# Pace and order of the S5 output work beside the gate projection, and the row pitch of its short kernels in DRAM

## The chip, the cores and the metric

The kernel runs on one core of one Trainium2 chip. A core has a matrix engine (TensorE, PE, with its weight loads PEld on a side path), a vector engine (VectorE, DVE), an activation engine (ScalarE, ACT), a general engine (GpSimd, POOL), and a queue engine (SyncE, SP) that issues most of the transfers between DRAM and on-chip memory (SBUF); matrix products collect in banks of PSUM. The metric is the time of one execution on the device in microseconds, the median of several runs.

## The reference

The program is a trunk of two sub-layers over 256 frames of width 2048: a gated linear attention and an S5 layer, each with modulation by a condition vector, a SiLU gate branch, an output projection and a LayerNorm. The change is in the S5 mixer alone:

```python
proj = u_in @ w_in                        # 2048 -> 2 x 4096
u, z = jnp.split(proj, 2, axis=-1)
...                                       # lb, bb: the discretised diagonal A and B
def blk(args):                            # 16 groups of 16 channels, 64 complex states each
    u_b, lr_b, li_b, br_b, bi_b, cr_b, ci_b = args
    bu_r = jnp.einsum('blgi,gpi->blgp', u_b, br_b)
    bu_i = jnp.einsum('blgi,gpi->blgp', u_b, bi_b)
    ...
    _, _, x_r, x_i = lax.associative_scan(_linear_recurrence_combine, (a_r, a_i, bu_r, bu_i), axis=1)
    return jnp.einsum('blgp,gip->blgi', x_r, cr_b) - jnp.einsum('blgp,gip->blgi', x_i, ci_b)
y = lax.map(blk, ...) + d_skip * uf
y = jax.nn.gelu(y)
y = y * jax.nn.sigmoid(y @ w_glu + b_glu)
y = y * jax.nn.silu(z)
return y @ w_out
```

All inputs and the output are float32.

## The kernel before

**Precision.** Each float32 weight tile is split into a high part `hi` (an ACT cast, line 145) and a low part `lo` (a DVE subtraction, line 146), and each product is made of three matmuls: high by high, high by low, low by high (lines 180, 181 and 182 in `st_step`; `u1h` and `u1l` are the parts of the layer's input, already in SBUF).

**The stages of the S5 layer.** First `su`: the columns of u, in 8 groups of 512. Beside it run the preparation of B and C, the first half of the scan, and the making of short kernels: the response of the recurrence inside 8 frames, one 16 x 1024 block for each of 32 f tiles (an f tile is 128 channels, 8 groups of 16). `k_out` writes these to a scratch array `dk` in DRAM, rows of 1920 floats, 16 rows for each f tile. Then comes `sz`: the gate columns z, again in 8 groups g of 8 steps kp; a step loads 512 KB of weights (`wload`, through SP; a ring of four tiles `wsz`), splits them (rings of three `hisz` and three `losz`) and issues 24 matmuls into four PSUM banks. The pool `mm` has five banks, so that a group's banks must be read by its four SiLUs (line 1280, `zs`) before the next group can go far. Last come `gl` (the GLU projection, lines 192 and 193, which needs y of all f tiles from its first step on), the output projection and the LayerNorm.

**The background list.** During groups 1 to 7 of `sz`, 56 steps, the program also finishes the scan's second half and makes y. A list `bg` holds closures; after each step's matmuls `pump(Y_RATE)` adds 2.311 to an account and calls one closure for each whole 1.0 in it. The closures are:

- `scan(cidx, 1)`, 30 of them: one step of the recurrence over chunks of 8 frames for the second half of the channels. Three DVE instructions, each needing the one before: a product (line 1183, into `sca`), a sum (1184), and a sum into the states `sx` (1185).
- `cside(f)`, 32 of them: `cload(f + 1)` issues three transfers of C and the powers of A (`cl`, two buffers, lines 1213 and 1215); `mload(f)` issues one transfer of 512 KB that spreads the short kernel of f from `dk` into a banded matrix `mt` (two buffers, line 1229): partition (i, s) reads 1024 consecutive floats of row i, beginning 128 floats later for each s. `cunit(f)` makes C times the powers, two DVE products (lines 1074 and 1075, tiles `wc`, two buffers each).
- `xstage(f)`: the states at the chunk starts, transposed by DVE (line 1237, `xT`, one buffer) and by PE (line 1240, `psxs`), and copied by ACT to `xS` (line 1242).
- `ystage(f)`: 24 small matmuls on PE into `psy`, 8 with `mt` on the inputs U (line 1252) and 16 with `wc` on the states `xS` (line 1255); then a DVE transpose `yt` (line 1258) and an ACT GELU that writes y over U (line 1259).

Tiles 16 to 31 belong to the scan's second half, which has to be complete before `xstage(16)`. For each f from 0 to 33 the list has up to three scans, then `cside(f)`, `xstage(f - 1)` and `ystage(f - 2)`: six entries while there are scans (ten tiles), three afterwards. Thirty scans, 32 `cside`, 32 `xstage` and 32 `ystage` are 126 entries. What is left at the end of the 56 steps is called ahead of `gl`.

**What sets the order in the end.** The program text gives each engine a first order, and the tile framework then places the instructions on each engine's queue anew by their dependences, so that the pieces of one closure may be apart from one another. The engine executes its queue strictly in that order. PE's next step waits for `hisz` and `losz`; a `psy` group waits for `mt`, `wc` and `xS`; a `mt` transfer waits for the `psy` group of two tiles before, which frees the buffer; SP's queue stands while its first transfer waits. The SiLU and the GELU use different tables of ACT's functions, and each change between them is a load on ACT.

Of the kernel before, what the change touches and what calls it, by code (L numbers as in the profile page):

```python
# [8 lines left out]
F32 = mybir.dt.float32  # L9
# [24 lines left out]
def trunk(ctx, tc, x, c, ln_g, ln_b, ada_w, ada_b, gla_w_in, gla_gate_w2, gla_gate_b, gla_norm_g,  # L34
# [7 lines left out]
    def pool(name, bufs=1, **kw):  # L42
        return ctx.enter_context(tc.tile_pool(name=name, bufs=bufs, **kw))
# [9 lines left out]
    dp = pool("dram", 1, space=DRAM)  # L53
# [23 lines left out]
    def psm(name):  # L77
        return mm.tile([P, 512], F32, tag="mm", name=name)

    def psx(name):  # L80
        return ax.tile([P, 512], F32, tag="ax", name=name)
# [10 lines left out]
    bg = []  # L92
# [3 lines left out]
    def pump(rate=1.0):  # L96
        pace[0] += rate
        while pace[0] >= 1.0:
            pace[0] -= 1.0
            if bg:  # L100
                bg.pop(0)()
# [28 lines left out]
    def less(got):  # L130
        for r, b in got:
            r.drop(b)
# [330 lines left out]

    rec = dp.tile([P, 32, 384], F32, name="rec")

    dk = dp.tile([512, 1920], F32, name="dk")
    dxn = dp.tile([T, D], F32, name="dxn")
    du = dp.tile([8, P, 1024], F32, name="du")

# [219 lines left out]
    KEEP = (4, 6)  # L689
    GATE_AT = 20  # L690
    SCAN_RATE = 1.728
    Y_RATE = 2.311
    qt, kt = qk
    gl = {}

# [352 lines left out]
    def Uv(f):  # L1048
        return Ut[f // 8][:, (f % 8) // 4, :, f % 4, :]
# [161 lines left out]
    def cload(f):  # L1211
        a = tp.tile([P, 384], F32, tag="cl", name=f"cl{f}", bufs=2)
        dma(a[:, 0:256], rec[:, f, 0:256])
        for h in range(2):
            dma(a[64 * h:64 * h + 64, 256:384], rec[64 - 64 * h:128 - 64 * h, f, 0:128])
        cl[f] = a
# [7 lines left out]
    kap = dk[:, :]  # L1224

    def mload(f):
        m = tp.tile([P, 8, 8, 16], F32, tag="mt", name=f"mt{f}", bufs=2)
        src = bass.AP(tensor=kap.tensor, offset=kap.offset + f * 16 * 1920, ap=[[1920, 16], [128, 8], [1, 1024]])
        dma(m.rearrange("p t g i -> p (t g i)"), src)
        mt[f] = m  # L1230

# [2 lines left out]
    def xstage(f):  # L1234
        xt_ = tp.tile([P, 2, 4, 32], F32, tag="xt", name=f"xT{f}", bufs=1)
        n = 2 * (f % 16)
        V.transpose(xt_, sx[:, f // 16, 0:32, :, n:n + 2].rearrange("p c r b -> p b r c"))
        px = psx(f"psxs{f}")
        for b in range(2):
            PE.transpose(px[:, b * P:(b + 1) * P], xt_[:, b].rearrange("p r l -> p (r l)"), ident)  # L1240
        xs = tp.tile([P, 2, 128], F32, tag="xs", name=f"xS{f}", bufs=2)
        S.copy(xs, px[:, :T].rearrange("p (b r) -> p b r", b=2))
        xss[f] = xs

    def ystage(f):
        xs = xss[f]
        py = psx(f"psy{f}")
        U = Uv(f)
        for b in range(2):
            o = py[:, b * P:(b + 1) * P]  # L1250
            for q in range(4):
                PE.matmul(o[32 * q:32 * q + 32], lhsT=U[:, 2 * q + b], rhs=mt[f][:, :, 2 * q + b, :], start=True, stop=False)
            for w in wc[f]:
                for q in range(4):
                    PE.matmul(o[32 * q:32 * q + 32], lhsT=xs[:, b, 32 * q:32 * q + 32],
                              rhs=w[:, 2 * q + b].rearrange("p n i -> p (n i)"), start=False, stop=(w is wc[f][-1]))
        yt = tp.tile([P, 8, 32], F32, tag="yt", name=f"yt{f}", bufs=2)
        V.transpose(yt, py[:, :T].rearrange("p (b t i) -> p t b i", b=2, t=8))
        S.activation(U, yt, AF.Gelu_apprx_tanh)

    def cside(f):
        if f < 31:
            cload(f + 1)
        mload(f)
        cunit(f)

    zs = []
    for g in range(8):
        banks = [psm(f"sz{g}{f}") for f in range(4)]
        for kp in range(8):  # L1270
            w = split(wload(sw, 2 * kp, E + g * 512, f"sz{g}{kp}"), f"sz{g}{kp}")
            st_step(banks, u1, w, kp, 15)
            if g == 0:
                bstep(1 + kp % 2)
            pump(SCAN_RATE if g == 0 else Y_RATE)
        for f in range(4):
            i = (g * 4 + f) % 8
            if g % 2 == 0 and f == 0:
                zs.append(s8t(f"zs{g // 2}", [8, T]))
            S.activation(zs[g // 2][:, i, :], banks[f][:, :T], AF.Silu)  # L1280
        if g == 0:
            bstep(len(bq))
            while bg:
                bg.pop(0)()
            less(mid)
            tp.close()
            tp.open("tmp2")
            cload(0)
            sc1 = [lambda cidx=cidx: scan(cidx, 1) for cidx in range(1, 31)]
            for f in range(34):  # L1290
                for _ in range(3):
                    if sc1:
                        bg.append(sc1.pop(0))
                if f < 32:
                    bg.append(lambda f=f: cside(f))
                if 1 <= f < 33:
                    bg.append(lambda f=f: xstage(f - 1))
                if f >= 2:
                    bg.append(lambda f=f: ystage(f - 2))
    while bg:  # L1300
        pump()

    tp.close()
    rp.open("rows1")
# [147 lines left out]
```

## Time and profile before

| | before |
|---|---|
| median of 3 runs | 1825.99 us |
| lowest, highest | 1824.85, 1827.47 us |
| the profiled execution's own time | 1828.37 us |
| its span in the profile | 1826.6 us |
| mean granted clock of TensorE in it | 0.992 |
| ACT: high parts of `sz`, mean of one | 1050 ns |
| `wsz`, 512 KB, issue to landing, all 64 | 5.7 us |
| `mt`, 512 KB, issue to landing, all 32 | 7.8 us |
| `zs`, SiLU of one bank, median | 384 ns |

A row of the profile's groups names the line, the engine, the operation, the tiles written and read, the shape, and how often it occurs; then the busy time, the mean of one, and the idle time of the engine just ahead of such instructions with what ended it. A row of the waits gives the waiting instruction, what released it, and then the sum of the idle time in microseconds, the number of waits and their mean. A row of the timeline has the start in microseconds from the span's start, the duration, the engine and the instruction, `x8` for eight alike in a row, and in square brackets the idle time ahead of it. The engines' times beside each other say which one sets the pace. The matmuls of `sz` run from 1016.9 to 1277.5 us of this execution, group 0 included.

### The profile page before, as it was taken

How to read it: one execution, taken by the hardware profiler on the slowest of the kernel's cores; microseconds unless marked ns; L12 is line 12 of the kernel's file. 1: busy time of each engine (PE TensorE's matmuls, PEld its weight loads, DVE VectorE, ACT ScalarE, POOL GpSimd, SP SyncE). 2: the span in 40 equal slices, each digit the busy share in tenths (PEclk: the TensorE clock that was granted, in tenths of full speed). 3: DMA queues.
4: the chain of work that ended last, by engine and by line, in shares of the span. 5: the costliest groups of instructions: out<-in, count | busy, mean ns of one | idle time of the engine just before them, and what ended most of it. 6: DMA issues, size and time to landing. Idle time of an engine off the chain costs nothing.

```text
span 1826.6 us, 33659 instructions
## 1 busy us (share of the span) xinstructions
PE 1780.4 (97%) x13491; PEld 1573.1 (86%) x13491; DVE 1411.3 (77%) x1880; ACT 898.9 (49%) x1266; POOL 86.3 (5%) x94
## 2 busy tenths in 40 slices
PE   7999999999999999999999999999999999999997
PEld 5776897899999888799999999989888888888885
DVE  4887757879999988687789789889577775557556
ACT  4433557556556333655555544546545444444332
POOL 0000000000000000002224300000000000000000
PEclk9999999999999999999999999999999999999998
DMA  9996975879889998587666577999788886668553
GB/s 344 387 358 229 296 249 163 277 265 324 288 285 323 331 364 290 175 254 212 193 199 191 171 223 211 242 241 239 227 283 267 275 275 200 189 200 316 195 183 92
DMA packets 246101, 457.86 MB, mean 251 GB/s; under 512 B 19828, under 2 KB 49198, under 8 KB 244662
## 3 DMA queue, kind: packets, MB, share of 16 engines
q1 hardware_dynamic: 239320, 436.02, 74.4%
q0 software_dynamic: 5856, 18.63, 3.1%
q8 instruction: 106, 1.74, 0.4%
q10 hardware_dynamic: 768, 1.05, 0.2%
q14 instruction: 51, 0.42, 0.1%
HBM read 437.01 MB, written 18.61 MB: 249 GB/s over the span
## 4 chain that ended last, share of the span: by engine, by line
PE 83%; DVE 6%; DMA 5%; ACT 3%; issue 3%; SPq 1%; POOL 0%; DVEq 0%; ACTq 0%; POOLq 0%
PE gl L192 13%; PE gl L193 7%; PE op L168 6%; PE op L169 6%; PE op L167 6%; PE v L168 3%; PE z L182 3%; PE z L181 3%; PE z L180 3%; PE v L169 3%; PE v L167 3%; PE sz L180 3%; PE sz L182 2%; PE su L180 2%; PE sz L181 2%
## 5 line engine op out<-in xcount | busy, mean ns | idle before, releaser
L146 DVE TENSOR_TENSOR logl<-wgl,higl 128x1024 fp32r<-128x1024 f32 x128 | 156.7, 1224 | 116.3 <-ACT higl L145 114.6
L145 ACT CAST higl<-wgl 128x1024 fp32r<-128x1024 f32 x128 | 134.3, 1050 | 172.2 <-PE gl L192 165.4
L192 PE MATMUL gl<-yp,higl 128*128 128x512 f32 x512 | 179.9, 396 | 0.1
L192 PE MATMUL gl<-yb,higl 128*128 128x512 f32 x512 | 179.6, 396 | 0.0
L145 ACT CAST hio<-wo 128x1024 fp32r<-128x1024 f32 x95 | 100.2, 1055 | 153.0 <-PE op L169 134.8
L146 DVE TENSOR_TENSOR loo<-wo,hio 128x1024 fp32r<-128x1024 f32 x95 | 116.7, 1230 | 66.4 <-ACT hio L145 64.5
L317 DVE SCALAR_TENSOR_TENSOR acc<-wa,cs,acc 128x512 f32<-128x512 f32 x217 | 163.0, 751 | 2.7
L180 PE MATMUL su<-u1h,hisu 128*128 128x256 f32 x512 | 151.4, 297 | 0.0
L180 PE MATMUL sz<-u1h,hisz 128*128 128x256 f32 x512 | 150.1, 293 | 1.2 <-ACT zs L1280 1.2
L180 PE MATMUL z<-u0h,hiz 128*128 128x256 f32 x512 | 148.7, 290 | 0.0
L182 PE MATMUL su<-u1h,losu 128*128 128x256 f32 x512 | 145.3, 284 | 0.4 <-DVE losu L146 0.4
L182 PE MATMUL sz<-u1h,losz 128*128 128x256 f32 x512 | 144.5, 283 | 1.1 <-DVE losz L146 1.1
L182 PE MATMUL z<-u0h,loz 128*128 128x256 f32 x512 | 144.9, 283 | 0.6 <-DVE loz L146 0.6
L181 PE MATMUL su<-u1l,hisu 128*128 128x256 f32 x512 | 145.1, 284 | 0.0
L181 PE MATMUL z<-u0l,hiz 128*128 128x256 f32 x512 | 144.7, 283 | 0.0
L181 PE MATMUL sz<-u1l,hisz 128*128 128x256 f32 x512 | 144.5, 282 | 0.0
L193 PE MATMUL gl<-yb,logl 128*128 128x256 f32 x512 | 143.0, 279 | 0.0
L193 PE MATMUL gl<-yp,logl 128*128 128x256 f32 x512 | 142.3, 280 | 0.0
L145 ACT CAST hisz<-wsz 128x1024 fp32r<-128x1024 f32 x64 | 67.0, 1050 | 108.4 <-PE sz L181 60.2
L192 PEld LDWEIGHTS gl<-yp,higl 128*128 128x128 f32 x512 | 95.9, 188 | 23.3 <-issue 0.8
L192 PEld LDWEIGHTS gl<-yb,higl 128*128 128x128 f32 x512 | 96.1, 188 | 23.0
L145 ACT CAST hiz<-wz 128x1024 fp32r<-128x1024 f32 x64 | 67.2, 1052 | 89.0 <-PE z L181 79.4
(322 smaller groups left out, 5001.1 us busy)
## 6 DMA issues: line engine op xcount, KB each, us to landing
wgl<-in_s_w_glu SPq DMA_DIRECT2D x128, 512.0 KB, 4.8
wa<-in_ada_w SPq DMA_DIRECT2D x116, 512.0 KB, 5.3
wv<-in_gla_w_in SPq DMA_DIRECT2D x64, 512.0 KB, 6.2
wz<-in_gla_w_in SPq DMA_DIRECT2D x64, 512.0 KB, 5.0
wsu<-in_s_w_in SPq DMA_DIRECT2D x64, 512.0 KB, 4.2
wsz<-in_s_w_in SPq DMA_DIRECT2D x64, 512.0 KB, 5.7
wo<-in_s_w_out SPq DMA_DIRECT2D x64, 512.0 KB, 4.5
a<-in_ada_w SPq DMA_DIRECT2D x31, 1024.0 KB, 10.8
```

What stands on the lines that cost most here:

```text
L145: S.copy(hi, w)
L146: last_lo[0] = V.tensor_tensor(lo, w, hi.bitcast(F32), op=ALU.subtract).ins
L167: PE.matmul(banks[tt], lhsT=uh, rhs=hi[:, kk, :], start=(k == first), stop=False)
L168: PE.matmul(banks[tt], lhsT=uh, rhs=lo[:, kk, :], start=False, stop=False)
L169: last_mm[0] = PE.matmul(banks[tt], lhsT=ul, rhs=hi[:, kk, :], start=False, stop=(k == last)).ins
L180: PE.matmul(o, lhsT=wh, rhs=u.hi(k), start=(k == first), stop=False)
L181: PE.matmul(o, lhsT=wh, rhs=u.lo(k), start=False, stop=False)
L182: last_mm[0] = PE.matmul(o, lhsT=wl, rhs=u.hi(k), start=False, stop=(k == last)).ins
L192: PE.matmul(banks[f], lhsT=hi[:, kk, fs], rhs=u.both(k), start=(k == 0), stop=False)
L193: PE.matmul(banks[f][:, :T], lhsT=lo[:, kk, fs], rhs=u.hi(k), start=False, stop=(k == last))
L317: V.scalar_tensor_tensor(acc[0], w[:, kk, :], cs[:, k:k + 1], acc[0], op0=ALU.mult, op1=ALU.add)
```

## The change

**The pitch.** `dk` has rows of 2048 floats in place of 1920, 8192 B in place of 7680. `k_out` writes and `mload` reads the same columns as before; 128 floats at each row's end stay unused.

**The list.** Groups 1 to 7 no longer use `bg` and `Y_RATE`. A list `yq` holds pairs of a weight and a closure: scan 1.0, `xstage` 1.0, `cside` 2.5, `ystage` 2.0. The sum of all weights is 30 + 32 + 2.5 x 32 + 2 x 32 = 206, and each of the 56 steps adds 206/56 = 3.68 to an account; closures are called while the account covers the first one's weight. For each f the list has two scans in place of three, so that the scans reach to the 15th tile, and `xstage(f - 1)` now stands ahead of `cside(f)`. Group 0 is as before.

```diff
@@ -463,7 +463,7 @@
 
     rec = dp.tile([P, 32, 384], F32, name="rec")
 
-    dk = dp.tile([512, 1920], F32, name="dk")
+    dk = dp.tile([512, 2048], F32, name="dk")
     dxn = dp.tile([T, D], F32, name="dxn")
     du = dp.tile([8, P, 1024], F32, name="du")
 
@@ -689,7 +689,6 @@
     KEEP = (4, 6)
     GATE_AT = 20
     SCAN_RATE = 1.728
-    Y_RATE = 2.311
     qt, kt = qk
     gl = {}
 
@@ -1225,7 +1224,7 @@
 
     def mload(f):
         m = tp.tile([P, 8, 8, 16], F32, tag="mt", name=f"mt{f}", bufs=2)
-        src = bass.AP(tensor=kap.tensor, offset=kap.offset + f * 16 * 1920, ap=[[1920, 16], [128, 8], [1, 1024]])
+        src = bass.AP(tensor=kap.tensor, offset=kap.offset + f * 16 * 2048, ap=[[2048, 16], [128, 8], [1, 1024]])
         dma(m.rearrange("p t g i -> p (t g i)"), src)
         mt[f] = m
 
@@ -1264,6 +1263,7 @@
         mload(f)
         cunit(f)
 
+    yq, owed = [], 0.0
     zs = []
     for g in range(8):
         banks = [psm(f"sz{g}{f}") for f in range(4)]
@@ -1272,7 +1272,13 @@
             st_step(banks, u1, w, kp, 15)
             if g == 0:
                 bstep(1 + kp % 2)
-            pump(SCAN_RATE if g == 0 else Y_RATE)
+            if g == 0:
+                pump(SCAN_RATE)
+            else:
+                owed += yrate
+                while yq and owed >= yq[0][0]:
+                    owed -= yq[0][0]
+                    yq.pop(0)[1]()
         for f in range(4):
             i = (g * 4 + f) % 8
             if g % 2 == 0 and f == 0:
@@ -1288,17 +1294,16 @@
             cload(0)
             sc1 = [lambda cidx=cidx: scan(cidx, 1) for cidx in range(1, 31)]
             for f in range(34):
-                for _ in range(3):
-                    if sc1:
-                        bg.append(sc1.pop(0))
+                yq.extend((1.0, sc1.pop(0)) for _ in range(2) if sc1)
+                if 1 <= f < 33:
+                    yq.append((1.0, lambda f=f: xstage(f - 1)))
                 if f < 32:
-                    bg.append(lambda f=f: cside(f))
-                if 1 <= f < 33:
-                    bg.append(lambda f=f: xstage(f - 1))
+                    yq.append((2.5, lambda f=f: cside(f)))
                 if f >= 2:
-                    bg.append(lambda f=f: ystage(f - 2))
-    while bg:
-        pump()
+                    yq.append((2.0, lambda f=f: ystage(f - 2)))
+            yrate = sum(w_ for w_, _ in yq) / 56
+    while yq:
+        yq.pop(0)[1]()
 
     tp.close()
     rp.open("rows1")
```

Line numbers of the changed kernel are one lower than before from `KEEP` to `cunit`, since the line of `Y_RATE` is gone. The order of the matmuls of one step, the transfers' sizes and all instructions are the same in both kernels; what differs is which instruction stands behind which. In the order of PE's queue, `psy` of tile 0 stands behind step 4 instead of step 6 (steps counted from 0 in groups 1 to 7), that of tile 10 behind step 25 instead of 28, that of tile 16 behind 35 in both, and that of tile 29 behind step 54 instead of 52.

Three places in the order of the queues follow. A row gives the line, the operation, the tile written and the tiles read (numbers tell buffers of the same name apart), and the shape.

The first is DVE's queue at the start of group 1, around the first two low parts behind the last `dk` writes. Before:

```order
L146 TENSOR_TENSOR losz_11541<-wsz_11538,hisz_11540 128x1024
L1185 TENSOR_TENSOR sx<-sx,sca_11444 128x128
L1074 TENSOR_TENSOR wc_11492<-cl_11406 128x1024
L1183 TENSOR_TENSOR sca_11448<-sx,l_205 128x256
L1075 TENSOR_TENSOR wc_11493<-cl_11406 128x1024
L1184 TENSOR_TENSOR sca_11448<-sca_11448 128x128
L1074 TENSOR_TENSOR wc_11574<-cl_11486 128x1024
L1185 TENSOR_TENSOR sx<-sx,sca_11448 128x128
L1075 TENSOR_TENSOR wc_11575<-cl_11486 128x1024
L1183 TENSOR_TENSOR sca_11452<-sx,l_205 128x256
L146 TENSOR_TENSOR losz_11592<-wsz_11589,hisz_11591 128x1024
```

The same place in the changed kernel, from the second `wc` product on:

```order
L1074 TENSOR_TENSOR wc_11489<-cl_11406 128x1024
L1183 TENSOR_TENSOR sca_11448<-sca_11448 128x128
L1073 TENSOR_TENSOR wc_11543<-cl_11482 128x1024
L1184 TENSOR_TENSOR sx<-sx,sca_11448 128x128
L1074 TENSOR_TENSOR wc_11544<-cl_11482 128x1024
L1182 TENSOR_TENSOR sca_11492<-sx,l_205 128x256
L1236 STREAM_TRANSPOSE xT_11585<-sx 128x256
L1183 TENSOR_TENSOR sca_11492<-sca_11492 128x128
L146 TENSOR_TENSOR losz_11595<-wsz_11592,hisz_11594 128x1024
```

The transpose of the first f tile and one more piece of a scan have moved ahead of the second low part; the four `wc` products stand there in both.

The second is DVE's queue at steps 17 to 19 of these 56. Before, from one low part to the next:

```order
L146 TENSOR_TENSOR losz_12369<-wsz_12366,hisz_12368 128x1024
L1074 TENSOR_TENSOR wc_12199<-cl_12076 128x1024
L1075 TENSOR_TENSOR wc_12200<-cl_12076 128x1024
L1258 STREAM_TRANSPOSE yt_12274<-psy_12249 128x256
L1183 TENSOR_TENSOR sca_12277<-sx,l_205 128x256
L1184 TENSOR_TENSOR sca_12277<-sca_12277 128x128
L1185 TENSOR_TENSOR sx<-sx,sca_12277 128x128
L146 TENSOR_TENSOR losz_12435<-wsz_12432,hisz_12434 128x1024
```

In the changed kernel, behind the two `wc` products of the tile at that place and up to the next low part:

```order
L1257 STREAM_TRANSPOSE yt_12230<-psy_12205 128x256
L1184 TENSOR_TENSOR sx<-sx,sca_12263 128x128
L1236 STREAM_TRANSPOSE xT_12393<-sx 128x256
L1182 TENSOR_TENSOR sca_12267<-sx,l_205 128x256
L1183 TENSOR_TENSOR sca_12267<-sca_12267 128x128
L1184 TENSOR_TENSOR sx<-sx,sca_12267 128x128
L1182 TENSOR_TENSOR sca_12385<-sx,l_205 128x256
L1183 TENSOR_TENSOR sca_12385<-sca_12385 128x128
L1184 TENSOR_TENSOR sx<-sx,sca_12385 128x128
L1182 TENSOR_TENSOR sca_12389<-sx,l_205 128x256
L1183 TENSOR_TENSOR sca_12389<-sca_12389 128x128
L146 TENSOR_TENSOR losz_12403<-wsz_12400,hisz_12402 128x1024
```

There the two `wc` products, one `yt` and three pieces of a scan stand between two low parts; here, behind the `wc` products, it is one `yt`, one `xT` and nine pieces of scans.

The third is PE's queue at the end of the stage. Before, the last `psy` group (tile 31; its second half reads alike), the last step of `sz` (only its first three and last matmul are shown) and the first matmul of `gl`:

```order
L1252 MATMUL psy_14643<-mt_14477,U_7548 32x128 x4
L1255 MATMUL psy_14643<-wc_14479,xS_14583 32x128 x4
L1255 MATMUL psy_14643<-wc_14480,xS_14583 32x128 x4
...
L180 MATMUL sz_14218<-u1h_7422,hisz_14673 128x256
L181 MATMUL sz_14218<-u1l_7424,hisz_14673 128x256
L182 MATMUL sz_14218<-u1h_7422,losz_14674 128x256
...
L182 MATMUL sz_14221<-u1h_7422,losz_14674 128x256
L192 MATMUL gl_14721<-yp_14717,higl_14727 128x512
```

In the changed kernel, the last matmuls of the last step, then `psy` of tiles 30 and 31 (first half of each), and the first matmul of `gl`:

```order
L180 MATMUL sz_14183<-u1h_7422,hisz_14617 128x256
L181 MATMUL sz_14183<-u1l_7424,hisz_14617 128x256
L182 MATMUL sz_14183<-u1h_7422,losz_14618 128x256
L1251 MATMUL psy_14645<-mt_14473,U_7548 32x128 x4
L1254 MATMUL psy_14645<-wc_14475,xS_14542 32x128 x4
L1254 MATMUL psy_14645<-wc_14476,xS_14542 32x128 x4
...
L1251 MATMUL psy_14677<-mt_14574,U_7548 32x128 x4
L1254 MATMUL psy_14677<-wc_14576,xS_14613 32x128 x4
L1254 MATMUL psy_14677<-wc_14577,xS_14613 32x128 x4
...
L192 MATMUL gl_14721<-yp_14717,higl_14727 128x512
```

The last group of tile 31 has moved from ahead of the last step of `sz` to behind it, and that of tile 30 stands with it, right ahead of `gl`.

## The prediction

> **What bounds the kernel now.** I read the page first: TensorE (PE) is busy for almost the whole span.
>
> ```profile
> span 1826.6 us, 33659 instructions
> PE 1780.4 (97%) x13491; PEld 1573.1 (86%) x13491; DVE 1411.3 (77%) x1880; ACT 898.9 (49%) x1266; POOL 86.3 (5%) x94
> ```
>
> The change touches the stretch in which PE computes the gate columns `sz` of groups 1 to 7 (56 steps of 24 matmuls) and, between the steps, the S5 output of 32 f tiles. By the trace it runs from about 1050 to 1278 us. The table by windows splits it where the scans end:
>
> ```profile
> core 0: us, PE busy (x) PEld busy (x) DVE busy (x) ACT busy (x) POOL busy (x), PEclk, DMA share, GB/s
> 1050.00:1140.00 90.00, 87.72 (x990) 84.52 (x993) 82.66 (x150) 41.48 (x63) 2.28 (x4) 1.00 0.78 219
> 1140.00:1278.00 138.00, 135.09 (x1972) 125.91 (x1965) 122.25 (x142) 74.95 (x119) 0.00 (x0) 1.00 0.96 239
> ```
>
> PE is idle for 2.28 us in the first part and 2.91 us in the second: 5.19 us. The change leaves every matmul in place and the granted clock is already 1.00, so **5.2 us, 0.28% of the span, is the most that can be won here**. What ended this idle time is in the list of PE's waits for the same stretch:
>
> ```profile
> PE psy L1252 <- DMA mt<-dk: 1.8, 3, 1.0
> PE sz L180 <- ACT zs L1280: 1.2, 2, 1.0
> PE psy L1252 <- ACT U L1259: 1.1, 1, 1.1
> PE sz L182 <- DVE losz L146: 1.1, 1, 1.1
> ```
>
> Four kinds, then. The one on `losz` stands at the start. VectorE (DVE) comes to this stage late, held 5.2 us by the landing of the last `dk` writes, and then has 7 us of other work between two low parts:
>
> ```profile
> 1055.05 0.43 DVE L1183 TENSOR_TENSOR sca<-sx,l 128x256 f32<-128x256 f32 x1 [5.20 <-DMA dk<-ks]
> ...
> 1056.11 1.22 DVE L146 TENSOR_TENSOR losz<-wsz,hisz 128x1024 fp32r<-128x1024 f32 x1
> ...
> 1063.06 1.23 DVE L146 TENSOR_TENSOR losz<-wsz,hisz 128x1024 fp32r<-128x1024 f32 x1
> ```
>
> The two on `zs` are at group boundaries: ScalarE (ACT) has a GELU (`U`) ahead of the SiLUs that free PE's banks, the GELU waits for DVE's `yt`, and the change of function table comes on top:
>
> ```profile
> 1105.48 0.42 ACT L1259 ACTIVATE U<-yt 128x256 f32<-128x256 f32 x1 [1.41 <-DVE yt L1258]
> 1105.92 1.28 ACT L1280 ACT_TABLE_LOAD   x1
> 1107.21 1.21 ACT L1280 ACTIVATE zs<-sz 128x256 f32<-128x256 f32 x4
> ```
>
> The 1.8 us are `mt` tiles that land late, and I count the 1.1 us on `U` with them: it is at one of the same places, where an `mt` landed within a microsecond of it. The chain of waits shows two such landings after the `psy` group that freed the buffer:
>
> ```profile
> 1157.44 8.76 DMA mt<-dk
> ...
> 1235.16 7.02 DMA mt<-dk
> ```
>
> **The change part by part.** No instruction is added or removed; only order and addresses change. The unit prices are distances between starts. On PE a step's matmuls start 0.12 us apart (24 x 0.12 = 2.88 us), `psxs` takes 0.31 and a `psy` group 1.45 us, 1.76 together:
>
> ```profile
> 1268.06 0.28 PE L180 MATMUL sz<-u1h,hisz 128*128 128x256 f32 x1
> 1268.18 0.28 PE L181 MATMUL sz<-u1l,hisz 128*128 128x256 f32 x1
> ...
> 1268.42 0.38 PE L1240 MATMUL psxs<-ident,xT 128*128 128x128 f32 x2
> 1268.73 0.43 PE L1252 MATMUL psy<-mt,U 128*32 128x128 f32 x8
> ...
> 1270.18 0.38 PE L180 MATMUL sz<-u1h,hisz 128*128 128x256 f32 x1
> ```
>
> On DVE:
>
> ```profile
> 1113.11 1.21 DVE L1074 TENSOR_TENSOR wc<-cl 128x1024 f32<-128x1024 f32 x1
> 1114.24 1.21 DVE L1075 TENSOR_TENSOR wc<-cl 128x1024 f32<-128x1024 f32 x1
> 1115.38 0.44 DVE L1258 STREAM_TRANSPOSE yt<-psy 128x256 f32<-128x256 f32 x1
> 1115.75 0.38 DVE L1183 TENSOR_TENSOR sca<-sx,l 128x256 f32<-128x256 f32 x1
> ...
> 1116.69 1.22 DVE L146 TENSOR_TENSOR losz<-wsz,hisz 128x1024 fp32r<-128x1024 f32 x1
> 1117.83 0.42 DVE L1183 TENSOR_TENSOR sca<-sx,l 128x256 f32<-128x256 f32 x1
> ...
> 1118.93 0.43 DVE L1183 TENSOR_TENSOR sca<-sx,l 128x256 f32<-128x256 f32 x1
> 1119.28 0.65 DVE L1237 STREAM_TRANSPOSE xT<-sx 128x256 f32<-128x256 f32 x1
> ```
>
> A low part is 1.14, the two `wc` 2.27, `yt` 0.37, `xT` 0.58 (0.65 less the overlap of 0.07 that the others have). A scan is 0.94 (1115.75 to 1116.69) to 1.10 (1117.83 to 1118.93).
>
> *The pace.* Before, a step takes 2.311 list entries. An f tile with three scans has six entries and lasts 2.60 steps; one without has three and lasts 1.30. Now the list weighs 30 + 32 + 80 + 64 = 206, so 3.68 a step: a tile with two scans (7.5) lasts 2.04 steps, one without (5.5) 1.50.
> - With scans, DVE per tile: before 3 x 0.94 to 1.10, + 3.22 + 2.60 x 1.14 = 9.0 to 9.5 us, beside 2.60 x 2.88 + 1.76 = 9.25 of PE; now 7.4 to 7.8 beside 7.64. **DVE is level with PE in both**, only longer: 15 tiles instead of 10. Here the pace gains nothing.
> - Without scans DVE has room in both: 4.7 beside 5.50, now 4.9 beside 6.07.
>
> *The transfers.* Per tile one `mt` (0.524 MB), three `cl` (0.197 MB), and 0.524 MB of weights a step:
>
> ```profile
> DMA packets 18261, 32.95 MB, mean 239 GB/s; under 512 B 1887, under 2 KB 7263, under 8 KB 18240
> wsz<-in_s_w_in SPq DMA_DIRECT2D x26, 512.0 KB, 9.4
> mt<-dk SPq DMA_DIRECT2D x23, 512.0 KB, 7.8
> cl<-rec SPq DMA_DIRECT2D x21, 128.0 KB, 7.8
> cl<-rec SPq DMA_DIRECT2D x42, 32.0 KB, 6.5
> ```
>
> That is 1140 to 1278 us. 239 GB/s at a share of 0.96 is a capacity of about 250. Without scans the need was 1.40 MB in 5.50 us, 255 GB/s: over it. Now it is 1.50 MB in 6.07 us, 248; with scans 1.79 MB in 7.64 us, 234. Also, `mt` of tile f can only be issued once `psy` of f-2 has read the buffer. In the old order these two groups are often two steps apart, 2 x 4.64 - 1.45 = 7.8 us for a landing of 7.8; in the new order three from tile 14 to 29, 2.88 more. So of 2.9 us I leave **0.3** (0 to 1.5).
>
> *The start.* In the new order DVE has one more `xT` and one more third of a scan between the two low parts (0.58 + 0.2), and PE has a `psxs` less to wait with: 1.1 becomes **1.7** (1.1 to 1.9).
>
> *One long stretch.* At steps 17 to 19 the new DVE order has `wc wc yt`, `xT` and nine pieces of scan ahead of one low part (2.27 + 0.37 + 0.58 + 9 x 0.35 + 1.14 = 7.5 us) and another 4.0 us ahead of the next, against PE's 2.88 + 0.31 and 2.88. DVE loses 5.4 us. Its lead is at most two low parts, about 4 to 5 us: before, it ran with it from 1070 to 1130 without one wait of PE on `losz`. So **1.0** (0 to 2.2).
>
> *The boundaries.* The GELU of a late tile stands ahead of the SiLUs now only after step 23, where before it did after steps 15 and 23. **0.2** of 1.2 stays (0 to 1.2).
>
> *The end.* The last three groups are bunched: `psy` of tile 29 after step 54, then one step, then 30 and 31 together, ahead of the first `gl` matmul. `mt` 31 waits for `psy` 29 and has 0.31 + 2.88 + 1.45 + some 0.5 = 5.2 us. Nothing but `mt` 30 is ahead of it in SP's queue. The lightest median in the trace is 7.1 (1050 to 1140 us), which would leave 1.9, with queues that this one does not meet:
>
> ```profile
> mt<-dk SPq DMA_DIRECT2D x9, 512.0 KB, 7.1
> cl<-rec SPq DMA_DIRECT2D x11, 128.0 KB, 2.9
> ```
>
> A quarter of the bytes lands in 2.9, so below I bound it by nothing; **0.7** (0 to 2.3).
>
> *The pitch.* Rows of `dk` are 8192 B apart instead of 7680; bytes and packets are the same. Nearest rows with rows of 8 KB (`s_w_out` and `gla_w_out`, 2048 floats) and of 16 KB (`w_glu`):
>
> ```profile
> wgl<-in_s_w_glu SPq DMA_DIRECT2D x128, 512.0 KB, 4.8
> wo<-in_s_w_out SPq DMA_DIRECT2D x64, 512.0 KB, 4.5
> big<-in_gla_w_out SPq DMA_DIRECT2D x23, 512.0 KB, 9.8
> ```
>
> 4.5 beside 4.8 says that 8 KB costs nothing, and I take **0**. The far ends: `mt` at 9.8 instead of 7.8 is 25% slower; and faster, which can at most remove the 0.3 and 0.7 above.
>
> The Trainium skill, page "DMA: Bandwidth & Descriptors", section "Latency and other measured facts", speaks against such a pitch: rows a large power of two apart copy more slowly, 207 GB/s at 512 KiB and 103 at 4 MiB, and a few KiB of padding restore it. It has no figure near 8 KiB, and the three rows above do not show the effect there. By the rule the sum would be that of the third rival below.
>
> *Sum.* 1.7 + 1.0 + 0.2 + 0.3 + 0.7 = 3.9 us of idle PE against 5.2: **-1.3 us**. The profiled execution took 1828.37 us (span 1826.6), 2.4 over the median of 1825.99; the median goes to 1824.7. All low ends give 1.1 left (-4.1, 1821.9), all high ends 9.1 (+3.9, 1829.9).
>
> **The rivals.** A measurement of this kernel can tell about 0.2%, 3.65 us, from no change.
> 1. *The even pace does what it says*: the waits at the boundaries, in the middle and at the end go, and the long stretch is covered. For it: DVE's lead of up to 5 us. Against: the order at step 17, and the bunched end. Left are 1.1 to 1.7 us: 1821.9 to 1822.5, say 1822.0.
> 2. *DVE becomes the wait* (the other side). Where scans run uninterrupted (1.10), DVE needs 7.8 beside 7.64 in all 15 tiles: 0.16 x 15 = 2.4 us more, and with no lead left the stretch costs 2.2, the boundary 1.2 and the start 1.9. With 0.3 and 0.7 this is 8.7: 1829.5. It decides as soon as a tile's DVE work passes 7.64. Against: nearly all scan pieces lie between other work.
> 3. *The 8 KB pitch slows `mt`.* `mt` is 12.1 of 32.95 MB, 37%, and the need of 248 leaves 1% of 250. So from 3% slower on, every further 10% costs 3.7% of some 104 us, 3.8 us; at 25%, 8.5: about 1833 (a halved rate would cost 35). For it: nothing in the trace; `wo` at 4.5 is against.
> 4. *The change does not do what it says*: the four waits stay as large in other places, 1826. This is inside my forecast's range.
>
> **How the numbers follow.** Forecast 1824.7 (1822.4 to 1828) with rival 4: 0.56. Rival 1: 0.21. Rival 2: 0.13. Rival 3: 0.10. Faster by over 0.2% (below 1822.3): most of rival 1 and the edge of the forecast, 0.20. Slower (above 1829.6): rival 3 and half of rival 2, 0.16. Within: 0.64. The range of 1821.0 to 1830.0 leaves out rival 3 and the outer ends of 1 and 2.
>
> **What would show it.** In the waits of PE for this stage: no more than 0.5 us on `mt` before the last tiles, one wait of 1.0 to 1.9 on `losz` at step 4 and a second at steps 18 to 19, at most one on `zs`, and a new one on `mt` or `psy` just ahead of the first `gl`. The stage's DMA rate should stay near 240 to 250 GB/s; a median landing of `mt` above 9 us would prove rival 3, one under 6 the opposite. The forecast is wrong if PE's idle time here is under 2 or over 7 us, or if a stage outside this one moves.

## The result and the profile after

The changed kernel takes 1821.93 us (median of 12 runs, 1819.75 to 1829.83) beside 1827.08 for the kernel before (12 runs): a ratio of 0.9974, interval 0.9963 to 0.9985. That is 2.7 to 6.8 us less, where 1.3 was forecast; the time itself lies inside the range. The profiled execution took 1820.42 us, its span is 1818.6.

The table by windows shows the stage of the change, with the columns as shown of before (PE, PEld, DVE, ACT and POOL busy, PEclk, DMA share, GB/s; the stage begins 1.3 us earlier here and ends at 1270 instead of 1277):

```profile
1050.00:1140.00 90.00, 88.84 (x1085) 84.93 (x1085) 85.12 (x148) 42.29 (x62) 1.70 (x3) 1.00 0.83 228
1140.00:1270.00 130.00, 130.00 (x1859) 123.22 (x1857) 116.68 (x139) 73.99 (x114) 0.00 (x0) 1.00 0.95 248
```

PE is idle for 1.16 us in the first part and for none in the second; before it was 2.28 and 2.91. In the first part DVE is busier (85.12 beside 82.66) and the DMA engines move more (228 GB/s beside 219): work has moved forward. PE's waits in this stretch are a single row (waiting instruction, releaser, then total, count and longest; the last figure of such a row is the longest wait, and not the mean as it is described ahead of the prediction):

```profile
PE psxs L1239 <- DVE xT L1236: 1.1, 1, 1.1
```

All four kinds of before are gone. The stage, from the first `sz` matmul of group 1 to the first `gl` matmul, took 226.9 us before and takes 220.7: **6.2 less, of which 4.0 are idle time**. The spans differ by 8.0. The u-projection ahead of the change's stage took 2.2 less, group 0 of `sz` behind it 0.7 more, and the remaining 0.3 lie elsewhere. In these two parts `pss` waits for inputs; before and after:

```profile
PE pss L1124 <- DMA U<-du: 2.6, 3, 1.9
```

```profile
PE pss L1123 <- DMA U<-du: 0.7, 1, 0.7
```

PE's idle time in the u-projection came out between 0.2 and 4.4 us in the profiles of this study, in one and the same kernel at 0.2 and 2.0; it belongs to the single execution and not to the change.

### The profile page after: what moved, and what is told of

Same layout as the page of the kernel before. It is cut to its first block, busy times and chain, and to the rows that moved or that the text cites. A ratio compares the mean times of both kernels' runs of the same rounds, so it can differ in the third digit from the quotient of the medians.

```text
span 1818.6 us, 33661 instructions
## 1 busy us (share of the span) xinstructions
PE 1778.2 (98%) x13491; PEld 1572.8 (86%) x13491; DVE 1410.1 (78%) x1880; ACT 900.1 (49%) x1267; POOL 89.1 (5%) x94
## 4 chain that ended last, share of the span: by engine, by line
PE 87%; DVE 6%; DMA 3%; issue 2%; ACT 2%; POOL 0%; SPq 0%; DVEq 0%; ACTq 0%; POOLq 0%
PE gl L192 13%; PE gl L193 7%; PE op L168 6%; PE op L169 6%; PE op L167 6%; PE su L180 3%; PE su L182 3%; PE su L181 3%; PE sz L180 3%; PE sz L182 3%; PE sz L181 3%; PE z L182 3%; PE z L181 3%; PE z L180 3%; PE v L168 3%; PE v L169 2%
## 5 line engine op out<-in xcount | busy, mean ns | idle before, releaser
L168 PE MATMUL v<-lov,u0h 128*128 128x512 f32 x256 | 102.9, 402 | 6.2 <-DVE lov L146 6.2
```

Of the source, the lines that this page charges most:

```text
L168: PE.matmul(banks[tt], lhsT=uh, rhs=lo[:, kk, :], start=False, stop=False)
```

## The experiments

Theory A: what removed the waits on `mt` is the even distance between `psy` groups, since two buffers hold each transfer back until `psy` of two tiles before is done. Theory B: the row pitch makes `mt` land sooner. Theory D: part of the gain is no waiting at all but the price of PE's changes between forms of matmul. The others are named where they arise. The table gathers what the runs gave. "Idle" is PE's in the stage; "waits" is measured between starts of matmuls (what a distance between two starts has clearly above the usual one of its kind), so that it also holds the last part of the matmul ahead, which idle time counts as busy; the last column is the stage less these waits. In e4 and e7 this column also holds some 1.1 us that PE lost at half its granted clock, as told at e4.

| kernel | ratio to before (interval) | stage | idle | waits | stage less waits |
|---|---|---|---|---|---|
| before | 1 | 226.9 | 5.2 | 6.2 | 220.7 |
| after | 0.9974 (0.9963 to 0.9985) | 220.7 | 1.2 | 1.6 | 219.1 |
| e1 pitch only | 1.0003 (0.9989 to 1.0017) | 227.2 | 5.7 | 6.5 | 220.7 |
| e2 list only | 0.9976 (0.9963 to 0.9989) | 222.4 | 2.5 | 3.3 | 219.1 |
| e3 weights only | 0.9996 (0.9982 to 1.0011) | 226.3 | 5.3 | 6.1 | 220.1 |
| e4 equal weights | 1.0005 (0.9991 to 1.0019) | 227.7 | 6.0 | 7.1 | 220.6 |
| e5 psy ahead | 1.0006 (0.9994 to 1.0018) | 225.6 | 4.0 | 4.8 | 220.9 |
| e6 even tail | 0.9982 (0.9967 to 0.9997) | 223.9 | 3.7 | 4.3 | 219.6 |
| e7 scan buffer | 0.9989 (0.9979 to 0.9999) | 224.2 | 2.9 | 3.4 | 220.8 |
| e8 after again | 0.9975 (0.9965 to 0.9985) | 223.6 | 3.6 | 4.6 | 219.0 |
| e9 before, more mt | 1.0004 (0.9996 to 1.0013) | 225.3 | 4.1 | 4.8 | 220.6 |
| e10 more mt | 0.9998 (0.9989 to 1.0008) | 225.4 | 5.4 | 6.3 | 219.2 |
| e11 later start | 1.0058 (1.0044 to 1.0073) | 234.5 | 12.1 | | |
| e12 third mt | 0.9987 (0.9978 to 0.9996) | 223.0 | 3.3 | 3.8 | 219.1 |

**e1, e2: pitch or list.**

```diff
-    dk = dp.tile([512, 1920], F32, name="dk")
+    dk = dp.tile([512, 2048], F32, name="dk")
...
-        src = bass.AP(tensor=kap.tensor, offset=kap.offset + f * 16 * 1920, ap=[[1920, 16], [128, 8], [1, 1024]])
+        src = bass.AP(tensor=kap.tensor, offset=kap.offset + f * 16 * 2048, ap=[[2048, 16], [128, 8], [1, 1024]])
```

e1 is the kernel before with this edit; e2 is the changed kernel with it undone.

> The kernel before with only the row pitch of dk changed from 1920 to 2048 floats; every queue stands in the order of before. Theory A (the distance between psy groups decides: an mt transfer may start only when psy of two tiles before has read the buffer, and with 7.7 to 9.2 us to the next use it lands late): nothing changes. PE idle between the first sz step of group 1 and the first gl matmul 4 to 6.5 us (before 5.2), waits on mt 1 to 4 us in all, time within 0.1% of before. Theory B (the pitch makes mt land sooner): waits on mt under 0.5 us, idle 2 us less, time 0.10 to 0.25% below before.

> The changed kernel with the old row pitch of 1920 floats; every queue stands in the order of the changed kernel. Theory A: all of the gain stays. PE idle in the stage 1.0 to 2.0 us (changed kernel 1.1), no wait on mt over 0.5 us, time 0.15 to 0.35% below before. Theory B: waits on mt of 1.5 us or more come back, and the time is within 0.1% of before.

The waits of PE in the stage, of e1 and then of e2:

```profile
PE psy L1252 <- DMA mt<-dk: 1.8, 3, 0.7
PE psy L1252 <- ACT U L1259: 1.4, 1, 1.4
PE sz L182 <- DVE losz L146: 1.2, 1, 1.2
PE sz L180 <- ACT zs L1280: 1.0, 2, 0.8
```

```profile
PE psxs L1239 <- DVE xT L1236: 1.3, 2, 1.1
PE psy L1251 <- DMA mt<-dk: 1.1, 1, 1.1
```

With the pitch alone the four kinds of before stand there in almost the same sizes and the time is unchanged; with the list alone all of the gain is there. B is out. The one wait on `mt` of e2 is ahead of the last tile, and larger than the 0.5 that was expected.

**e3, e4: which part of the list.** e3 keeps the weights and takes back the rest; e4 keeps the rest and takes back the weights:

```diff
-                yq.extend((1.0, sc1.pop(0)) for _ in range(2) if sc1)
+                yq.extend((1.0, sc1.pop(0)) for _ in range(3) if sc1)
-                if 1 <= f < 33:
-                    yq.append((1.0, lambda f=f: xstage(f - 1)))
                 if f < 32:
                     yq.append((2.5, lambda f=f: cside(f)))
+                if 1 <= f < 33:
+                    yq.append((1.0, lambda f=f: xstage(f - 1)))
```

```diff
-                    yq.append((2.5, lambda f=f: cside(f)))
+                    yq.append((1.0, lambda f=f: cside(f)))
...
-                    yq.append((2.0, lambda f=f: ystage(f - 2)))
+                    yq.append((1.0, lambda f=f: ystage(f - 2)))
-            yrate = sum(w_ for w_, _ in yq) / 56
+            yrate = 2.311
```

> The changed kernel with three scans per f tile and cside ahead of xstage, as before; so the weighted account alone (and the pitch). From step 29 on its psy groups stand behind the same steps as in the changed kernel. Theory A: no wait on mt over 0.5 us, idle 1.0 to 2.5 us, time 0.10 to 0.35% below before. Rival C (it is the two scans per tile or the place of xstage that removed the waits): idle 3 us or more, with waits on losz in steps 5 to 24, where a tile still holds three scans in some 2.3 steps; time within 0.1% of before.

> The changed kernel with all weights 1.0 and the old rate of 2.311; two scans per tile and xstage ahead of cside stay. Its psy groups from tile 12 on stand behind steps 31, 32, 33, 35, 36, 37, 38, 40 and so on, three of them in three steps, as before. Theory A: waits on mt of 1 to 4 us, idle 3 to 6 us, time within 0.12% of before. Rival C: no wait on mt over 0.5 us, idle under 2 us, time 0.15 to 0.35% below before.

The waits of e3, then those of e4:

```profile
PE psy L1251 <- DMA mt<-dk: 2.7, 1, 2.7
PE sz L182 <- DVE losz L146: 1.8, 2, 1.2
PE sz L180 <- ACT zs L1286: 0.5, 1, 0.5
PE psxs L1239 <- DVE xT L1236: 0.4, 1, 0.4
```

```profile
PE psy L1251 <- DMA mt<-dk: 3.8, 2, 3.4
PE sz L182 <- DVE losz L146: 1.1, 1, 1.1
PE sz L180 <- ACT zs L1286: 1.1, 1, 1.1
```

Neither half keeps the gain. In e3 the waits on `mt` in the middle are gone, as A says, but one of 2.7 stands ahead of the last tile, which follows the one two before by a single step, and waits on `losz` and `zs` are back, as rival C of the expectation has it; the expected idle time was 1.0 to 2.5 and it is 5.3. In e4 the waits on `mt` are back, as A says. The large one is at tile 24, two steps behind tile 22: its turn was 8.3 us after `psy` of tile 22 had freed the buffer, and its transfer took 11.6 us from its issue. Six other tiles of e4 (14, 17, 18, 21, 27 and 28) come two steps behind the tile two before and do not wait. So the landing itself varies, and the distance only sets how much of that is covered. Over the ten profiles with two buffers this holds as well: of 17 waits on `mt` over 0.1 us, 16 are at tiles that come two steps or one behind the tile two before. The old order has 11 such tiles, the new one two, the last ones.

The wait of e4 had a second price. Its rows of PE, and the table of the 3.41 us that follow (columns as above):

```profile
1234.10 0.28 PE L182 MATMUL sz<-u1h,losz 128*128 128x256 f32 x1
1237.82 0.43 PE L1251 MATMUL psy<-mt,U 128*32 128x128 f32 x8 [3.44 <-DMA mt<-dk]
...
1239.82 0.41 PE L181 MATMUL sz<-u1l,hisz 128*128 128x256 f32 x1
1240.04 0.41 PE L182 MATMUL sz<-u1h,losz 128*128 128x256 f32 x1
```

```profile
1239.04:1242.45 3.41, 3.41 (x26) 3.04 (x19) 2.28 (x2) 0.42 (x2) 0.00 (x0) 0.50 0.58 161
```

The granted clock was 0.50 there instead of 1.00, and twelve `sz` matmuls start 0.21 us apart instead of 0.12: 1.1 us more.

**e8: the changed kernel once more**, without an edit.

> The changed kernel once more, for a second profile of it. If the gain is what the first one showed, the stage takes 220.5 to 223 us, with one wait of 1.0 to 1.4 us on xT at step 2 and none on mt ahead of the last two tiles; the wait for the last mt is anywhere from 0 to 1.5 us. The u-projection ahead of it, where the profiles so far had 0.2 to 3.1 us of idle PE whatever the kernel, may come out anywhere in that range. Time 0.15 to 0.35% below before.

Its waits of PE in the stage:

```profile
PE psy L1251 <- DMA mt<-dk: 2.4, 3, 1.0
PE psxs L1239 <- DVE xT L1236: 1.1, 1, 1.1
```

The wait on `xT` is the same to a tenth, the waits on `mt` are not: none in the first profile, 2.4 us in this one, one of them (1.0) at step 39, which was not expected: tile 19 comes three steps behind tile 17. The first profile of the changed kernel was a lucky one: the stage took 220.7, 222.4 (e2) and 223.6 us in three profiles of this order, 226.9 and 227.2 in two of the old order. The mean difference is 4.8 us, and the timings of after, e2 and e8 (0.9974 to 0.9976) say 4.4 to 4.8.

**e9, e10, e12: more places for mt.** The scan's state tile is no longer read in its first half after tile 15, so `mt` can stand there, without new space. e9 is the kernel before, e10 the changed one, with four such places and the transfer issued one tile sooner; e12 is the changed kernel with one such place and no advance:

```diff
+        if f < 18:
             m = tp.tile([P, 8, 8, 16], F32, tag="mt", name=f"mt{f}", bufs=2)
+        else:
+            k = f % 4
+            m = sx_[:, k * 1024:(k + 1) * 1024].rearrange("p (t g i) -> p t g i", t=8, g=8)
...
-        mload(f)
+        if f < 18:
+            mload(f)
+        if 17 <= f < 31:
+            mload(f + 1)
```

```diff
+        if f < 18 or f % 3:
             m = tp.tile([P, 8, 8, 16], F32, tag="mt", name=f"mt{f}", bufs=2)
+        else:
+            m = sx_[:, 0:1024].rearrange("p (t g i) -> p t g i", t=8, g=8)
```

> The kernel before, whose mt tiles from tile 18 on stand in four places of the first half of the scan's state tile (no longer read by then) instead of the two mt buffers, and are issued one tile sooner; matmuls and their order are those of before. Theory A (the two buffers hold the transfer back, and where the next use is 8 us away it lands late): waits on mt and U from step 38 on go; left are losz 1.1, zs 1.0 to 1.2 and at most 0.5 on mt at steps 26 to 37; idle 2.2 to 4 us (before 5.2, pitch alone 5.7), time 0.05 to 0.2% below before. Rival G (the DMA engines can't deliver more in this stretch, 255 GB/s wanted against some 250): mt or wsz lands late all the same, idle 4.5 us or more, time within 0.05% of before.

> The changed kernel with the same four places for mt from tile 18 on. Theory A: the waits on mt that the changed kernel shows in some runs (0, 1.1 and 2.4 us in three profiles) go; idle 1.1 to 1.8 us, stage 220.5 to 221.5 us, time 0 to 0.15% below the changed kernel and 0.25 to 0.45% below before. Rival G: waits of 1 us or more on mt, wsz or cl stay.

> The changed kernel with one place more for mt from tile 18 on (every third tile stands in the first half of the scan's state tile), without the one tile of advance, so that SP's queue stays almost as in the changed kernel and no burst of mt transfers goes ahead of wsz and cl at steps 33 to 37, as it did in the two kernels with four places. Theory A: no wait on mt over 0.3 us after step 36, where the two profiles of the changed kernel and the one with the old pitch had 0, 2.4 and 1.1 us; idle 1.1 to 1.8 us, stage 220.5 to 221.5 us, time 0 to 0.15% below the changed kernel, 0.25 to 0.45% below before. Rival G (the engines' rate is the limit): waits of 0.5 us or more on mt stay after step 36, and the time is that of the changed kernel or above.

The waits of e9, then those of e12:

```profile
PE sz L180 <- ACT zs L1287: 1.5, 2, 1.4
PE psy L1256 <- DMA mt<-dk: 1.5, 2, 1.2
PE sz L182 <- DVE losz L146: 1.1, 1, 1.1
```

```profile
PE psy L1254 <- DMA mt<-dk: 2.2, 1, 2.2
PE psxs L1242 <- DVE xT L1239: 1.1, 1, 1.1
```

The waits on `mt` that are left lie at steps 34 and 35 in e9, 33 in e12 and 36 in e10, at tiles 15 to 17, which still use the two buffers. After step 37 there is none in these three kernels nor in e11, while seven of the ten profiles with two buffers have one to four of them over 0.1 us there. So the buffers, and not the engines' rate, hold `mt` back there. Rival G is out for these steps; its time for e9 (no change) and its wait of 1 us or more in e10 did come, the latter at tile 17. In e10 and e12 these tiles come three steps behind the tile two before, so that three steps do not always cover a landing either. As improvements the three are misses. In e9 and e10 the first transfers to the new places went out in a burst at steps 33 to 37, ahead of weights and `cl`, and in e10 waits of 3.2 us (1.5 on `mt`, 1.7 on `xS`) stand there at step 36. In e12 this burst is gone, but idle time is 3.3 instead of 1.1 to 1.8 for the one landing at step 33, and 0.9987 is no better than the changed kernel's 0.9974. Why it isn't as good, with the stage at 223.0, is open.

**e6: an even tail.**

```diff
-                    yq.append((2.5, lambda f=f: cside(f)))
+                    yq.append((2.5 if f < 16 else 2.3, lambda f=f: cside(f)))
...
-            yrate = sum(w_ for w_, _ in yq) / 56
+            yrate = 206 / 56
```

> The changed kernel with the weight of cside 2.3 instead of 2.5 from tile 16 on, at the same rate of 3.68, so that psy of tiles 28 to 31 stands behind steps 52, 53, 54 and 55 instead of 53, 54, 55 and 55. Theory A with the bunched end (the wait for the last mt hangs on how fast it lands: 0 us in the changed kernel, 1.1 and 2.7 in two of the runs with the same end): no wait on mt over 0.5 us at the end, idle 1.0 to 1.8 us, time as the changed kernel within 0.1%. Rival: two steps between psy of f - 2 and of f at the end are too short as well, and two or three waits of 0.3 to 1 us on mt take the place of the one, idle 2 us or more.

The waits on `mt` of e6:

```profile
PE psy L1251 <- DMA mt<-dk: 2.5, 2, 1.6
```

The rival was right: one wait of 1.6 where tiles 16 to 18 had come to stand behind steps 35, 36 and 37, and one of 0.9 behind step 54.

**e7, e11: the start.** e7 is e6 with the scans' scratch tile in a buffer of its own; e11 is e10 with a later start of the account:

```diff
-        t1 = tp.tile([P, 2, 2, 64], F32, tag="sc1", name=f"sca{cidx}{h}", bufs=1)
+        t1 = rp.tile([P, 2, 2, 64], F32, tag="sc1", name=f"sca{cidx}{h}", bufs=1)
```

```diff
-    yq, owed = [], 0.0
+    yq, owed = [], -3.68
```

> As the kernel with the even tail, and the scans' scratch tile sca stands in a buffer of its own instead of the space that the last transfers to dk are read from, so that scans need not wait for these. Theory F (the one wait left in the changed kernel, 1.1 us of PE on xT, comes from DVE standing 5 us for the last dk writes at the start of group 1): DVE runs its first scans in that time, PE waits under 0.4 us at steps 2 to 4, idle in the stage 0.1 to 0.9 us, DVE's lead at steps 18 to 27 is larger than in the changed kernel; time 0.05 to 0.1% below the changed kernel, which the timing hardly tells. Rival: the wc products need the same space, DVE waits there, and PE's wait stays at 1 us or more.

> As the one before, and the account starts at -3.68, so that the list starts one step later and ends with three psy groups behind the last step. Theory F (PE's 1.1 us on xT at step 2 come from DVE starting late): with a step more the wait falls to 0 to 0.6 us, the three bunched groups cost no wait since their mt are there, and idle is 0.1 to 1.2 us; time within 0.1% of the kernel without the delay. Rival: DVE still stands 5 us for the dk writes ahead of its low parts, so that the wait only moves to losz, 1.0 us or more.

In e7 DVE no longer stands for the last `dk` writes; it runs eight scans there, up to 1058 us. But four `wc` products come after them in one piece, and PE waits 1.9 us on the second tile's `xT` instead of 1.1: a miss. Then 0.4 on `losz` follow and, as in e4, 3.41 us at a granted clock of 0.50 (from 1065.3 us on). That is why its last column is 220.8, where e6 with the same order on PE has 219.6. In e11 the wait only moved to `losz` at step 4, and the rest is the reverse of a gain (waits of e11):

```profile
PE psxs L1243 <- DVE xT L1240: 6.0, 3, 5.3
PE sz L182 <- DVE losz L146: 4.4, 2, 3.3
```

The 3.3 are at step 26: one step less for the scans, and DVE is late. The 5.3 are at step 37, behind the burst of e10. Toward the ends of these two waits the granted clock went to 0.50, for 3.41 and 6.83 us, a part of what makes e11 the slowest.

**e5: turnarounds.**

```diff
-                if 1 <= f < 33:
-                    bg.append(lambda f=f: xstage(f - 1))
                 if f >= 2:
                     bg.append(lambda f=f: ystage(f - 2))
+                if 1 <= f < 33:
+                    bg.append(lambda f=f: xstage(f - 1))
```

> The kernel before with one edit: in the list, ystage(f - 2) stands ahead of xstage(f - 1), so that where both follow one step PE runs psy, then psxs, then sz, as the changed kernel does at 22 tiles. Old rate, old pitch, three scans, equal weights. Theory D (about 1.6 of the 6.2 us that the stage lost are not waits but turnarounds between forms of matmul: sz to psy 0.21, psy to psxs 0.20, psxs to sz 0.03 against sz to psxs 0.12, psxs to psy 0.20, psy to sz 0.20 and a slow second sz matmul): the stage's time less its waits falls by 0.8 to 1.8 us, from 220.7 to about 219 to 220, wherever the waits go; the waits on mt stay, 1 to 4 us, since psy groups are still as little as two steps apart. Rival E (the 1.6 us are cover that each wait costs beside its idle time): without fewer waits the time less waits stays within 0.4 us of before.

The waits on `mt`, expected at 1 to 4 us, are absent from this profile, though ten of its tiles come two steps behind the tile two before: an old pace can be lucky too, and the time is no better for it. The stage less its waits is 220.9, where E had put it. But three of its `psy` groups stand in two pieces with `sz` matmuls between, which cost about what the new order won, so the sum decides nothing. E falls by the other rows of the table: after, e2 and e8 have 1.6, 3.3 and 4.6 us of waits and the same 219.0 to 219.1 without them. That number goes with the order of PE's queue, not with the waits.

## Why the prediction was right and wrong

The measured time lies inside the range, but the gain is 4.8 us in the mean of the profiles, where 1.3 was forecast. **The step that failed** is in the prediction's list of unit prices: "`psxs` takes 0.31 and a `psy` group 1.45 us, 1.76 together", whatever stands beside them, and from it that "5.2 us, 0.28% of the span, is the most that can be won here". The changes between forms of matmul have a price, and the new order pays less. The timeline of PE shows it in the old kernel at three places (a `psxs` alone, a `psy` group alone, and `psxs` ahead of `psy`; start, duration, instruction):

```profile
1210.55 0.28 PE L182 MATMUL sz<-u1h,losz 128*128 128x256 f32 x1
1210.67 0.38 PE L1240 MATMUL psxs<-ident,xT 128*128 128x128 f32 x2
1210.80 0.36 PE L180 MATMUL sz<-u1h,hisz 128*128 128x256 f32 x1
1211.01 0.28 PE L181 MATMUL sz<-u1l,hisz 128*128 128x256 f32 x1
...
1213.64 0.28 PE L182 MATMUL sz<-u1h,losz 128*128 128x256 f32 x1
1213.85 0.43 PE L1252 MATMUL psy<-mt,U 128*32 128x128 f32 x8
...
1215.52 0.28 PE L181 MATMUL sz<-u1l,hisz 128*128 128x256 f32 x1
...
1218.15 0.28 PE L182 MATMUL sz<-u1h,losz 128*128 128x256 f32 x1
1218.27 0.38 PE L1240 MATMUL psxs<-ident,xT 128*128 128x128 f32 x2
1218.58 0.43 PE L1252 MATMUL psy<-mt,U 128*32 128x128 f32 x8
...
1220.25 0.28 PE L181 MATMUL sz<-u1l,hisz 128*128 128x256 f32 x1
```

and in the changed kernel, where `psy` stands ahead of `psxs`, and at the end, where two `psy` groups follow each other:

```profile
1225.82 0.28 PE L182 MATMUL sz<-u1h,losz 128*128 128x256 f32 x1
1226.03 0.42 PE L1251 MATMUL psy<-mt,U 128*32 128x128 f32 x8
...
1227.48 0.44 PE L1239 MATMUL psxs<-ident,xT 128*128 128x128 f32 x2
1227.67 0.36 PE L180 MATMUL sz<-u1h,hisz 128*128 128x256 f32 x1
1227.87 0.28 PE L181 MATMUL sz<-u1l,hisz 128*128 128x256 f32 x1
```

```profile
1267.22 0.28 PE L182 MATMUL sz<-u1h,losz 128*128 128x256 f32 x1
1267.43 0.43 PE L1251 MATMUL psy<-mt,U 128*32 128x128 f32 x8
...
1270.19 0.50 PE L192 MATMUL gl<-yp,higl 128*128 128x512 f32 x1
```

From the last `sz` ahead to the second one behind, less 0.24 for the two distances that would be there anyway: `psxs` alone 0.22, `psy` alone 1.64, together 1.86; `psxs` ahead of `psy` also 1.86; `psy` ahead of `psxs` 1.81. Two `psy` in one go, to the first matmul behind and less 0.12, take 2.85 instead of 3.28. The new order has 22 tiles with `psy` ahead of `psxs` where the old had 2, which gives 20 x 0.05 = 1.0, and the pair at the end gives 0.4: 1.4 of the 1.6 us by which the two orders differ without waits. Of the 0.4 the stage's end hides 0.1: the second `gl` matmul starts 0.34 us behind the first in the changed kernel and 0.23 before. The other 0.2 of the 1.6 are waits that the table's measure misses. With every distance counted that is more than 0.05 us over the usual one, the stage less its waits is 220.2 to 220.3 in the three profiles of PE's old order (before, e1, e9) and 218.8 in the five of the new one (after, e2, e8, e10, e12), 1.4 apart. The Trainium skill, page "TensorEngine Tiling (Array Packing)", section "Key Properties", says that a change of tiling mode drains TensorE. The rows agree, with 0.21 us from `sz` (128 x 128) to `psy` (128 x 32) and 0.20 back; the page gives no price.

**The idle time** was forecast at 3.9 us in sum; the three profiles of the new order (after, e2, e8) show 1.2, 2.5 and 3.6, the two of the old one 5.2 and 5.7. Term by term:

- *The start*, 1.7 (1.1 to 1.9): 1.1 in all three, the low end. The mechanism was right, but the place was one instruction off: PE waits on the second `xT` instead of on `losz`, and with that wait made, `losz` costs only 0.2 us more between starts.
- *The long stretch*, 1.0 (0 to 2.2): no idle time, 0.16 us between starts. DVE lost its lead as worked out, and the lead was a little larger than the 4 to 5 us that it was put at. Timeline of DVE, then of PE, of the changed kernel:

```profile
1106.92 1.22 DVE L146 TENSOR_TENSOR losz<-wsz,hisz 128x1024 fp32r<-128x1024 f32 x1
...
1114.29 1.22 DVE L146 TENSOR_TENSOR losz<-wsz,hisz 128x1024 fp32r<-128x1024 f32 x1
...
1118.26 1.18 DVE L146 TENSOR_TENSOR losz<-wsz,hisz 128x1024 fp32r<-128x1024 f32 x1
```

```profile
1113.37 0.28 PE L182 MATMUL sz<-u1h,losz 128*128 128x256 f32 x1
...
1116.46 0.28 PE L182 MATMUL sz<-u1h,losz 128*128 128x256 f32 x1
...
1119.21 0.28 PE L181 MATMUL sz<-u1l,hisz 128*128 128x256 f32 x1
1119.50 0.39 PE L182 MATMUL sz<-u1h,losz 128*128 128x256 f32 x1
```

  The low parts of steps 17 to 19 end at 1108.14, 1115.51 and 1119.44; PE takes them up at 1113.37, 1116.46 and 1119.50. A lead of 5.2 us is used up at step 19: there PE starts 0.28 us behind the matmul ahead, instead of 0.12, and idle time doesn't show it. e11 shows what stands behind it: a step less, and a wait of 3.3 at step 26.
- *The boundaries*, 0.2: 0, as the GELUs come at other steps. The two halves, e3 and e4, still have 0.5 and 1.1 there, and no run tests the GELUs' place by itself.
- *The middle and the end*, 0.3 and 0.7: 0, 1.1 and 2.4 in the three profiles, 1.2 in the mean. That is the right size, and it is chance: the last transfer, of tile 31, landed 4.4, 6.1 and 6.4 us after its issue.
- *The pitch*, 0: right (e1, e2). The packets of `mt` took 266 ns in the mean both before and after. The landings of the table before, 7.8 us, say less: the profile holds only three of them, and twelve in the changed kernel (median 7.4).

Of the rivals, the first (the pace does what it says, 1822.0) is what came, at a chance of 0.21. Its time was met, but with more idle time than it allowed and with the turnarounds that it didn't know, so in part by luck. The waits in the table fell from 6.2 and 6.5 to 1.6, 3.3 and 4.6, by 3.2 in the mean; with the 1.6 of the last column this is the 4.8 us that stage and timing show. By kind, in idle time, the waits on `mt` (with the one on `U`) fell from 2.9 and 3.2 to 1.2 in the mean, those at the boundaries from 1.2 and 1.0 to none, and the start stayed. The forecast of 1.3 was wrong by size: it left out the second part, it counted idle time where each of the seven waits costs some 0.15 us more between starts, and it took middle values for the start and the stretch, of which the trace in the end showed the low ones. The second rival's mechanism (DVE becomes the wait) is real and near: its lead is used up at step 19.

By the prediction's own signs the forecast did not do well. Idle time under 2 us was to show it wrong: the first profile has 1.2, the three 2.4 in the mean. The waits on `losz` at step 4 and steps 18 to 19 came as 0.2 and 0.16 us only, e8 has 1.0 on `mt` at tile 19 where at most 0.5 was allowed ahead of the last tiles, and the new wait ahead of `gl` came in two profiles of three.

## What to carry to other kernels

When work of one engine moves between work of another form, price it with its turnarounds: take the distance from the last matmul of the main stream to the second one behind the insert, in each order, not the insert's own length. A transfer into two buffers is as good as the shortest distance between two uses; here an even pace gained what more buffers at the old pace (e9, with the burst that they brought) did not, and it needs no space. A wait of some us can cost more than its length: look at the granted clock behind it. And one profile of such a stage is one draw: three profiles of the same order had 0 to 2.4 us of waits on the same transfers.

## What the runs showed of the hardware that was not expected

- Between `sz` and `psy` matmuls 0.20 to 0.21 us lie between starts at each change, where two `sz` are 0.12 apart, and 0.05 us depend on whether a `psxs` stands ahead of or behind the `psy` group; why the second is so no run here shows.
- A transfer of 512 KB from `dk` took from 4.4 us (the last one of the changed kernel, beside little else) to 11.6 us (e4, step 46) from its issue; the mean time of one of its packets of 4096 B was 256 to 277 ns in the ten profiles with two buffers, 256 the one with the list and the old pitch.
- With a wait of PE of 3.44 us (e4), two of 1.95 and 0.43 close together (e7), and one of 3.34 and one of 5.35 (e11) the granted clock went to 0.50 for 3.41 us (6.83 with the last); with single waits of 2.16 (e12) and 2.67 (e3) it stayed at 1.00. What decides this no run here shows.
